# Layer B of a two-layer streaming encoder: head pair 0 turned by DMA like the others, turns issued behind the query copies, the sample's value product in another bank, inverse sums and scans later

## The chip, the cores and the metric

The kernel runs on one core of one Trainium2 chip. A core has a matrix engine (TensorE, "PE" in the profile, with its weight loads shown apart as "PEld"), three engines for elementwise work (VectorE "DVE", ScalarE "ACT", GpSimd "POOL") and SyncE ("SP"), which here issues nearly all DMAs, in order, from one queue. Each engine works through its own list of instructions and waits for the others by semaphores. The metric is the device time of one execution in microseconds; the time shown is the median of a few runs.

## The reference

Two layers with a residual; the second one (layer B) is where the change lies.

```python
def project(x, norm_g, w_in, q_g, k_g, n_heads, n_kv):
    h = rms_norm(x, norm_g)
    q, k, v, gate = split(h @ w_in)          # per head of 64
    return rms_norm(q, q_g), rms_norm(k, k_g), v, gate

def attend(q, k, v, bias, valid, sinks):
    s = q @ k.T * 64 ** -0.5 + bias
    s = where(valid, s, -1e30)
    p = softmax(s)                           # layer A has sinks in the sum
    return p @ v

def gated_attention_layer(...):
    o = attend(...)                          # prompt: in chunks of 64 frames
    y = x + (o * silu(gate)) @ w_out
```

The prompt has 2048 frames, the sample 64 frames with a cache of 256. The width is 1024. Layer A has 16 query heads over 2 key heads and sees the own chunk of 64 and 2 earlier ones; layer B has 16 heads of its own and sees the own chunk and 8 earlier ones, with a learned bias by clipped distance.

## The kernel before

**Tiling.** Layer A runs first, then layer B. Layer B goes through its heads in 8 head pairs (`hp` 0 to 7). Within a head pair it goes through nine units in the order 0 to 6, sample, 7: a prompt unit is 256 frames, two tiles of 128; the sample is one unit of 64. Each unit has a projection (q, k, v and gate of this head pair, on PE at L706 to L708) and an attention. The projections of a later unit are cut into small pieces by the class `Filler` and put between the steps of the attention, so that PE has work while the softmax of a step goes through DVE and ACT. Small jobs of DVE, ACT and POOL (the low halves of queries and keys, of values, the gate, the inverse sums, weight preparation) are kept in the class `Background`: `put` queues one, `share` runs a part of them after each step, `run` runs one at once because its result is wanted. `tick` counts the shares. A job that has run in a share is tied behind the newest `anchor` of its engine, an instruction of the current step's softmax.

**What sets the order.** PE's order is the order in which the program is written. The lists of the other engines and of SP are set by a scheduler from the dependences; `behind(a, b)` and the anchors add "not before b on this engine".

**One attention step** (`pipeline`, function `scores`) is one head `h` of one tile `i`. PE multiplies queries by keys into one of two "sb" banks of PSUM (L1487 the high halves, L1488 the low). DVE adds the bias and takes the negative maximum `nm` (L1491), ACT takes the exponential and its sum `sm` (L1500). The weights `p` then have to be turned, keys on partitions, for the product with the values:

- In head pairs 1 to 7 (`turned`) DVE first adds a constant to `nm` (L1496), ACT makes a 16-bit high half (L1545), POOL the low half (L1546), and SP turns both with one DMA transpose (L1554, tile `pt`), issued a step later. Four steps after the score PE multiplies them by the values (`turned_products`, L1648).
- In head pair 0, and for the sample, PE transposes `p` in blocks of 128x128 into an "sb" bank (L895 in `values`), ACT and DVE split the result (L867, L868), and PE multiplies by the values in `products` (L1687), for the sample in `sample_outputs` (L1606, L1607).

After both heads, `gates` transposes the gate times the inverse sums (`G`, L895) and `finish` gathers the output: ACT L1302, DVE L1306, POOL L1307 and a store (L1314). Products and output stand in the one "o" bank. The sample's product also takes the "o" bank, after `run_all` of two lists of small jobs.

`queries` prepares the next unit: PE transposes q and k into the one "tp" bank, ACT writes the high halves (L1426, L1427), DVE the low halves (L1438, L1442), and SP copies the queries to the other half of the partitions (L1431, `q<-q`; issued by `flush` at the next step). `inverse` takes the reciprocal of the four sums (DVE L1519) and multiplies it into the gate (POOL L1530). It is put in the background when the scores of a unit's last step are written, and runs at the latest in `gates`.

**Scans.** Weights are scaled to 16 bit by their largest value, found a head pair ahead: a block of 512 columns is loaded (L182) and reduced (DVE L175); L231 and L190 collect the maxima.

**Head pair 0 alone** also makes the normed rows x1 for all head pairs: loads (L571), a row scale (POOL L587), ACT L590 and POOL L591 split them in two halves, and a store (L602) puts them in memory, from where the other head pairs read them.

## Time and profile before

| | before |
|---|---|
| median of three runs | 2196.76 us (2193.1 to 2198.49) |
| the profiled execution, its own time | 2200.77 us |
| its span in the profile | 2199.0 us |
| POOL L591 (x1 halves, whole span) | 184.1 us in 144 |
| POOL L1546 (low halves of turned weights) | 283.5 us in 224 |
| DMA transposes pt<-values | 224 |

A row of waits says which engine waited for what: total, times and longest in us. A row of a group gives busy time and the mean length of one in ns, then the idle time before it and who ended it. A timeline row gives start, length, engine, line and operation, and in brackets the idle time before it with its releaser. A DMA issue row ends with the median time from issue to landing. Head pair 0 of layer B's attention runs from 901.80 to 1062.60 us, the seven others from there to 2045.

### The profile page before, as it was taken

Reading aid. Unit: us, or ns where it says so; the run is one execution under the profiler, and the core shown is the slowest. Engines: PE = TensorE matmul, PEld = TensorE weight load, DVE = VectorE, ACT = ScalarE, POOL = GpSimd, SP = SyncE. Lnnn points to the kernel's source line nnn. Section 1 sums busy time; section 2 is a strip of 40 time slices with the busy share of each in tenths; the row PEclk is TensorE's granted clock in tenths of the full one; section 3 lists DMA queues with packets and bytes.
Section 4 is the critical chain, followed back from the end, with each engine's and each line's share of the span. In section 5 each row is a group of like instructions: output and inputs, shape, how many; then the busy total and the mean of one; then the engine's idle time right before and its main releaser. Section 6 shows DMA issues by size and latency. Waiting matters only on the chain.

```text
span 2199.0 us, 40839 instructions
## 1 busy us (share of the span) xinstructions
PE 2074.1 (94%) x12951; PEld 1476.7 (67%) x12951; DVE 1503.6 (68%) x4049; ACT 1428.2 (65%) x3610; POOL 1149.4 (52%) x1621
## 2 busy tenths in 40 slices
PE   7999999999999999899998999989999899899899
PEld 6887788878879998455554555545555455456788
DVE  6668778667676456678676686776867867577542
ACT  6878878767786333566666676766767668577420
POOL 5554544434454355754566575665756667465000
PEclk9999999999999999999999999999999999999999
DMA  8756546766545677635488696786867969568663
GB/s 267 260 173 215 184 128 212 212 181 195 176 123 162 201 216 218 221 113 195 115 190 212 142 209 170 184 222 142 209 180 168 231 129 207 146 139 187 203 206 122
DMA packets 512120, 404.96 MB, mean 184 GB/s; under 512 B 303696, under 2 KB 449376, under 8 KB 511872
## 3 DMA queue, kind: packets, MB, share of 16 engines
q1 hardware_dynamic: 511904, 402.35, 67.5%
q8 instruction: 102, 1.67, 0.3%
q14 instruction: 114, 0.93, 0.1%
HBM read 257.59 MB, written 73.43 MB: 151 GB/s over the span
## 4 chain that ended last, share of the span: by engine, by line
PE 52%; DVE 15%; DMA 12%; ACT 8%; POOL 6%; issue 5%; SPq 2%; ACTq 0%; POOLq 0%; DVEq 0%
PE pj L706 8%; PE pj L708 8%; PE pj L707 8%; PE pj L1856 5%; PE pj L1858 5%; PE pj L1857 5%; DMA wraw<-in_w_in_b_dram 4%; DVE p L1491 2%; PE sa L895 2%; POOL values L1546 2%; PE o L1648 2%; DVE pa L811 2%; DMA xraw<-in_x_rows_dram 2%; PE tp L895 2%; DMA wraw<-in_w_o_b_dram 1%
## 5 line engine op out<-in xcount | busy, mean ns | idle before, releaser
L706 PE MATMUL pj<-wh,xx 128*128 128x512 f16 (+2 forms) x1648 | 647.5, 393 | 5.8 <-ACT pb L729 2.2
L708 PE MATMUL pj<-wh,xx 128*128 128x512 f16 (+2 forms) x1648 | 628.8, 382 | 0.6 <-POOL xx L591 0.6
L707 PE MATMUL pj<-wh,xx 128*128 128x512 f16 x1024 | 395.3, 386 | 0.8 <-DVE wh L496 0.8
L1500 ACT ACTIVATE p<-p,nm 128x640 f32<-128x640 f32 (+5 forms) x264 | 199.6, 756 | 272.2 <-DVE nm L1496 218.1
L1546 POOL TENSOR_TENSOR values<-p,values 128x640 f16<-128x640 f32 (+2 forms) x224 | 283.5, 1266 | 157.9 <-ACT values L1545 155.4
L1856 PE MATMUL pj<-xx,wh 128*128 128x264 f32 (+1 forms) x1024 | 290.8, 284 | 5.5 <-DVE res L1866 2.7
L1857 PE MATMUL pj<-xx,wh 128*128 128x264 f32 (+1 forms) x1024 | 287.9, 281 | 0.0
L1491 DVE CUSTOM_DVE_ANT_0 p<-sb,BT 128x640 f32<-128x640 f32 (+5 forms) x272 | 195.5, 719 | 64.8 <-PE sb L1488 61.4
L707 PE MATMUL pj<-wl,xx 128*128 128x512 f32 (+1 forms) x624 | 234.7, 376 | 2.9 <-DVE wl L496 2.8
L591 POOL TENSOR_TENSOR xx<-xraw,xx 128x528 fp32r<-128x528 f32 (+4 forms) x144 | 184.1, 1297 | 91.3 <-ACT xx L590 84.1
L806 POOL TENSOR_TENSOR f<-f,mhalf 128x4 f32<-128x4 f32 (+2 forms) x187 | 191.4, 1024 | 12.9
L1307 POOL TENSOR_TENSOR o<-gt,o 128x256 f32<-128x256 f32 (+1 forms) x132 | 106.1, 804 | 165.0 <-ACT p L1210 91.4
L708 PEld LDWEIGHTS <-xx 128*128 128x128 f16 x1024 | 101.8, 99 | 127.5 <-issue 9.6
L811 DVE TENSOR_TENSOR pa<-pa,f 128x256 f32<-128x256 f32 (+3 forms) x221 | 143.3, 648 | 37.1 <-POOL f L806 32.4
L1210 ACT ACTIVATE p<-p,nm 128x257 f32<-128x257 f32 (+2 forms) x272 | 134.3, 497 | 50.5 <-DVE nm L1204 44.5
L788 POOL TENSOR_TENSOR sq<-pa 128x256 f32<-128x256 f32 (+2 forms) x187 | 114.3, 611 | 99.1 <-ACT pa L742 61.2
L706 PEld LDWEIGHTS <-xx 128*128 128x128 f16 x1024 | 101.8, 99 | 86.0 <-issue 5.7
L707 PEld LDWEIGHTS <-xx 128*128 128x128 f16 x1024 | 101.6, 99 | 81.7 <-issue 6.5
L1545 ACT CAST values<-p 128x640 f16<-128x640 f32 (+2 forms) x224 | 147.3, 658 | 6.5 <-DMA pt<-values 0.7
L1858 PE MATMUL pj<-xx,wl 128*128 128x264 f32 x512 | 145.4, 284 | 1.0 <-DVE wl L489 1.0
L1204 DVE CUSTOM_DVE_ANT_0 p<-sa,BT,nsink 128x256 f32<-128x256 f32 (+2 forms) x272 | 117.4, 468 | 38.6 <-PE sa L895 30.8
L1858 PE MATMUL pj<-xx,wh 128*128 128x264 f16 x512 | 142.1, 277 | 0.1
(273 smaller groups left out, 5032.0 us busy)
## 6 DMA issues: line engine op xcount, KB each, us to landing
xx<-xsb SPq DMA_DIRECT2D x112, 512.0 KB, 4.3
xx<-xsa SPq DMA_DIRECT2D x88, 512.0 KB, 4.9
xraw<-oga SPq DMA_DIRECT2D x64, 264.0 KB, 3.6
xraw<-ogb SPq DMA_DIRECT2D x64, 264.0 KB, 4.0
xsa<-xx SPq DMA_DIRECT2D x32, 512.0 KB, 4.1
wl<-in_w_in_b_dram SPq DMA_DIRECT2D x64, 256.0 KB, 4.9
wraw<-in_w_in_b_dram SPq DMA_DIRECT2D x56, 256.0 KB, 4.4
xraw<-in_x_dram SPq DMA_DIRECT2D x40, 256.0 KB, 4.0
```

Of the source, the lines that this page charges most:

```text
L591: nc.gpsimd.tensor_tensor(lo, rv, wide(hi), op=ALU.subtract)
L706: nc.tensor.matmul(ps[:n, :C], xh, wh, start=k == 0, stop=False)
L707: nc.tensor.matmul(ps[:n, :C], xh, wl, start=False, stop=False)
L708: nc.tensor.matmul(ps[:n, :C], xl, wh, start=False, stop=k == KC - 1)
L806: nc.gpsimd.tensor_tensor(fv, fv, mhalf[:n, :H], op=ALU.pow)
L811: nc.vector.tensor_tensor(sv, sv, fv.unsqueeze(2).to_broadcast([n, H, HD]), op=ALU.mult)
L1491: mi = nc.vector.tensor_tensor_reduce(out=p[r, :nk], in0=S[r, o : o + nk], in1=b, op0=ALU.add, op1=ALU.min, scale=1.0, scalar=3e38, accum_ ...
L1500: ex = nc.scalar.activation(p[:n, :nk], p[:n, :nk], AF.Exp, scale=-1.0, bias=it.nm[:n, c : c + 1], accum_out=it.sm[:n, c : c + 1],)
L1546: lo = nc.gpsimd.tensor_tensor(two[:, :, 1, :], pv, two[:, :, 0, :], op=ALU.subtract)
L1856: nc.tensor.matmul(ps[:, :OT], wh, oh, start=k == 0, stop=False)
L1857: nc.tensor.matmul(ps[:, :OT], wh, ol, start=False, stop=False)
L1858: nc.tensor.matmul(ps[:, :OT], wl, oh, start=False, stop=k == KC - 1)
```

## The change

1. `turned` no longer asks for `hp > 0`: the prompt units of head pair 0 are turned by DMA too. With it the delay `late` in `then`, the bank in `gates` and one scale become the same for all head pairs. In head pair 0, 140 PE transposes of 128x128 fall away, and 168 products move from L1687 to L1648; 32 DVE low halves (L868) go and 32 constants (L1496) come; ACT has 32 copies in place of 32 splits; POOL gets 32 subtractions (12 of the 16 per head at 640 columns), SP 32 DMA transposes.
2. A turn is tied behind the last copy of queries on SP.
3. The sample's product goes to the "tp" bank, and so no longer runs the two lists first.
4. `inverse` is put in the background one share later, after the last step's own.
5. The reductions of `scan` are tied behind the anchor of their engine. A background job may ask for a number of shares to pass (`wait`); the low half of v and the product of the gate ask for two.

```diff
--- before.py
+++ after.py
@@ -172,9 +172,11 @@
     def scan(i=None, keep=0):
         while len(pending) > keep:
             j, raw = pending.pop(0)
-            nc.vector.tensor_reduce(
+            r = nc.vector.tensor_reduce(
                 most[:, j : j + 1], raw, axis=AX.X, op=ALU.max, apply_absolute_value=True
             )
+            if r.ins.engine in bg.anchors:
+                behind(r.ins, bg.anchors[r.ins.engine])
             scanned.append(j)
         if i is not None:
             raw = t("wraw", [P, 512], WB) if keep else t("scan", [P, 512], 1)
@@ -237,7 +239,7 @@
         powers(row[:, h : h + 1], e, r)
         times(o[:, 0:1], r, WB_)
         times(o[:, 1:2], e, 1 / (HB * WB_))
-        times(o[:, 2:3], e, 0.5 / VB if h > 0 and len(TURNED) == 2 else 0.5 / (VB * PB))
+        times(o[:, 2:3], e, 0.5 / VB)
 
     def input_scales(h):
         everywhere(h, row[:, 20:23])
@@ -389,9 +391,10 @@
             self.queue, self.anchors, self.cost, self.lazy = [], {}, 0.0, False
             self.tick = 0
 
-        def put(self, cost, fn, urgent=False, lazy=False, weights=False, after=None):
+        def put(self, cost, fn, urgent=False, lazy=False, weights=False, after=None, wait=1):
             it = Item()
             it.fn, it.cost, it.urgent, it.weights, it.after = fn, cost, urgent, weights, after
+            it.wait, it.born = wait, self.tick
             if urgent:
                 self.queue.insert(sum(q.urgent for q in self.queue), it)
             else:
@@ -432,7 +435,9 @@
                     break
                 if it.fn is None or it.weights and most == 0:
                     continue
-                if it.after is not None and (it.after.fn is not None or it.after.tick == self.tick):
+                if it.after is not None and it.after.fn is not None:
+                    continue
+                if self.tick < it.wait + (it.after.tick if it.after is not None else it.born):
                     continue
                 most -= it.weights
                 budget -= it.cost
@@ -750,7 +755,7 @@
                 vh[:, :, HD:P], v, c, vh[:, :, 0:HD], op0=ALU.mult, op1=ALU.subtract
             )
 
-        held["rest"].append(bg.put(0.2, low, True))
+        held["rest"].append(bg.put(0.2, low, True, wait=2))
         held["evac"] = nc.scalar.activation(g, ps[:, 384:512], AF.Identity, scale=C_B(hp)).ins
         return a
 
@@ -833,7 +838,7 @@
         if not apart:
             return [bg.put(0.3, curve)]
         first = bg.put(0.2, curve)
-        return [first, bg.put(0.2, product, after=first)]
+        return [first, bg.put(0.2, product, after=first, wait=2)]
 
     def split_v(n, src, vt):
         sv = src.rearrange("p (h d) -> p h d", d=HD)
@@ -1428,7 +1433,7 @@
 
             def copies():
                 for hh, rows in enumerate(halves):
-                    load(wide(q1[hh][halves[1 - hh]]), wide(q1[hh][rows]))
+                    held["copy"] = load(wide(q1[hh][halves[1 - hh]]), wide(q1[hh][rows])).ins
 
             if it not in its[-2:]:
                 held["later"].append(copies)
@@ -1505,14 +1510,8 @@
             if turned(it, h):
                 parts(it, i, h, p, nk // P)
             if c == w - 1:
-                def fn():
+                if u == NU:
                     inverse(it, n, w)
-
-                item = bg.put(0.8, fn, True)
-                if u != NU:
-                    it.inverse = item
-                    return
-                bg.run(item)
 
         def inverse(it, n, w):
             u, T, tiles = it.unit
@@ -1535,7 +1534,7 @@
                 )
 
         def turned(it, h):
-            return it.unit[0] != NU and it.hp > 0 and h in TURNED
+            return it.unit[0] != NU and h in TURNED
 
         def parts(it, i, h, p, m):
             held["turn"] = r = (held["turn"] + 1) % 3
@@ -1551,9 +1550,10 @@
             if i == 0:
                 it.ph[h] = t("pt", [P, 2 * HALF], 2, F16)
             m = two.shape[1]
-            nc.sync.dma_start_transpose(
+            turn = nc.sync.dma_start_transpose(
                 it.ph[h][:, HALF * i : HALF * i + m].rearrange("p (c q) -> p c q", q=P), two
             )
+            behind(turn.ins, held["copy"])
 
         def values(it, i, h, short):
             u, T, tiles = it.unit
@@ -1581,13 +1581,15 @@
             ))
 
         def then(it, i, h):
-            late = it.hp > 0 and len(TURNED)
+            late = len(TURNED)
             if it.unit[0] == NU:
                 return [
                     (1, "values", (it, i, h)), (2 + late, "call", lambda: sample_outputs(it)),
                     (3 + late, "call", lambda: sample_turned(it)),
                 ]
             last = i == len(it.unit[2]) - 1
+            if (i, h) == (1, 1):
+                it.inverse = bg.put(0.8, lambda: inverse(it, P, 4), True)
             if turned(it, h):
                 two = it.two[i]
                 todo = [(1, "call", lambda: turn_p(it, i, h, two))]
@@ -1600,7 +1602,7 @@
             return psum("o", 512, 1)
 
         def sample_outputs(it):
-            O = o_bank()
+            O = tp_bank()
             for c in range(3):
                 vs = VS[:, c].rearrange("p h d -> p (h d)")
                 nc.tensor.matmul(O[:, 0:256], it.ph[0][:, c, 0:P], vs, start=c == 0, stop=False)
@@ -1657,7 +1659,7 @@
             u, T, tiles = it.unit
             n = tiles[0][2]
             bg.run(it.inverse)
-            GT = psum_b("sb", 1024, 2) if it.hp and len(TURNED) else tp_bank()
+            GT = psum_b("sb", 1024, 2)
             for e, (_, t0, _) in enumerate(tiles):
                 transpose(GT[:, t0 : t0 + n], it.G[:n, e * P : (e + 1) * P])
             it.gt = gate_t(GT[:, :T].rearrange("p (j s) -> p j s", j=1), T, G_B(it.hp))
```

SyncE's list in head pair 0, in the middle of its units, before (L571 loads and L602 stores x1, L1431 copies queries, L182 loads weights for a scan, L1314 stores an output):

```order
L571 DMA xraw_12564<-x_98 128x2x256
L1431 DMA q_2514_12428<-q_2514_12428 64x256 x2
L182 DMA wraw_12774<-in_w_o_b_dram 128x512
L1314 DMA ogb<-o_2511_12409 128x256
L571 DMA xraw_12805<-x_98 128x2x64
L602 DMA xsb<-xx_12586 128x2048
```

The same place with the change, where the lines are five higher (L576 and L607 are x1, L1436 the copies, L1553 a turn):

```order
L1436 DMA q_2497_12394<-q_2497_12394 64x256 x2
L607 DMA xsb<-xx_12333 128x2048
L1553 DMA_TRANSPOSE pt_12376<-values_11645 128x10x128
L576 DMA xraw_12523<-x_98 128x2x256
L184 DMA wraw_12708<-in_w_o_b_dram 128x512
L1553 DMA_TRANSPOSE pt_12474<-values_11645 128x10x128 x2
L1319 DMA ogb<-o_2508_12471 128x256
L1553 DMA_TRANSPOSE pt_12595<-values_11645 128x10x128
L576 DMA xraw_12746<-x_98 128x2x64
```

The turns stand behind the copies and between the loads and stores of x1.

VectorE's list at the end of head pair 2, just ahead of the sample's product, before:

```order
L1438 SCALAR_TENSOR_TENSOR q_1_111<-tp_17245,qf,q_3402_17250 64x256
L1442 SCALAR_TENSOR_TENSOR KB<-tp_17245,kf,KB 64x256
L175 TENSOR_REDUCE most<-wraw_17661 128x1
L231 TENSOR_TENSOR most<-most,gain 128x8
L190 TENSOR_REDUCE top<-most 128x1
L1491 ISA p_17321,nm_17146<-sb_17320,BT 128x640
L1491 ISA nm_17146 128x1
L811 TENSOR_TENSOR pa_17238<-pa_17238,f_17268 128x256
L1306 TENSOR_TENSOR o_3414_17310<-o_17192,o_3414_17310 64x256 x2
L831 SCALAR_TENSOR_TENSOR pb_17108<-sq_17291,pb_17108 128x128
```

And with the change (L1447 is the low half of the keys, L1496 the bias and maximum, L816 and L836 small jobs of the projection, L1311 the last read of the "o" bank):

```order
L1447 SCALAR_TENSOR_TENSOR KB<-tp_17121,kf,KB 64x256
L1496 ISA p_17197,nm_17022<-sb_17196,BT 128x640
L1496 ISA nm_17022 128x1
L816 TENSOR_TENSOR pa_17114<-pa_17114,f_17143 128x256
L1311 TENSOR_TENSOR o_3366_17186<-o_17066,o_3366_17186 64x256 x2
L175 TENSOR_REDUCE most<-wraw_17015 128x1
L836 SCALAR_TENSOR_TENSOR pb_16984<-sq_17167,pb_16984 128x128
```

The reduction of the scan (L175) moved from ahead of the step's softmax to behind it and behind the last read of the "o" bank; the collecting of the maxima is no longer here.

GpSimd's list around one unit of head pair 0, before (L587, L591 x1; L788, L805, L806 row norms; L1530 inverse sums into the gate):

```order
L1530 TENSOR_TENSOR G_12261<-pb_11760,sm_12078 128x128 x2
L788 TENSOR_TENSOR sq_12312<-pa_12294 128x256
L587 TENSOR_TENSOR xraw_12324<-xraw_12324,rows_12320 128x512
L587 TENSOR_TENSOR xraw_12328<-xraw_12328,rows_12320 128x512
L591 TENSOR_TENSOR xx_12349<-xraw_12324,xx_12349 128x512
L805 TENSOR_TENSOR f_12313<-f_12313,small 128x4
L806 TENSOR_TENSOR f_12313<-f_12313,mhalf 128x4
L591 TENSOR_TENSOR xx_12349<-xraw_12322,xx_12349 128x512
L591 TENSOR_TENSOR xx_12357<-xraw_12326,xx_12357 128x512
L591 TENSOR_TENSOR xx_12357<-xraw_12328,xx_12357 128x512
L788 TENSOR_TENSOR sq_12445<-pa_12418 128x256
```

And with the change (L592, L596 x1; L793, L810, L811 row norms; L1545 the low half of the weights to be turned):

```order
L592 TENSOR_TENSOR xraw_12304<-xraw_12304,rows_12300 128x512
L592 TENSOR_TENSOR xraw_12308<-xraw_12308,rows_12300 128x512
L810 TENSOR_TENSOR f_12295<-f_12295,small 128x4
L1545 TENSOR_TENSOR values_11645<-p_12277,values_11645 128x5x128
L596 TENSOR_TENSOR xx_12325<-xraw_12302,xx_12325 128x512
L596 TENSOR_TENSOR xx_12333<-xraw_12306,xx_12333 128x512
L596 TENSOR_TENSOR xx_12325<-xraw_12304,xx_12325 128x512
L811 TENSOR_TENSOR f_12295<-f_12295,mhalf 128x4
L1545 TENSOR_TENSOR values_11645<-p_12345,values_11645 128x5x128
L596 TENSOR_TENSOR xx_12333<-xraw_12308,xx_12333 128x512
L793 TENSOR_TENSOR sq_12410<-pa_12384 128x256
L810 TENSOR_TENSOR f_12411<-f_12411,small 128x4
```

Four low halves per unit now stand among the halves of x1 (two of them in these rows).

## The prediction

> **What bounds the kernel now.** I read the page first, for the engines' shares and the chain of waits; then the busy time of each engine by stretch, one for each head pair of layer B; then the waits of TensorE (PE) in the seven head pairs 1 to 7; last the timeline around the places that the change touches. The page:
>
> ```profile
> span 2199.0 us, 40839 instructions
> PE 2074.1 (94%) x12951; PEld 1476.7 (67%) x12951; DVE 1503.6 (68%) x4049; ACT 1428.2 (65%) x3610; POOL 1149.4 (52%) x1621
> PE 52%; DVE 15%; DMA 12%; ACT 8%; POOL 6%; issue 5%; SPq 2%; ACTq 0%; POOLq 0%; DVEq 0%
> ```
>
> PE is busy 94% of the span, and the chain that ended last runs through it for 52%. The time can fall in two ways: PE gets less to do, or its stalls (6%, and what hangs on them) get shorter. The change does the first in head pair 0 and means to do the second in the others.
>
> The next view gives busy time by stretch; the columns are the stretch, its length, PE, weight loads, DVE, ACT and POOL busy (instructions), the granted clock, DMA share and GB/s. The rows are head pair 0, its units 0 to 4, its rest (units 5, 6, the sample, 7), and the same rest of head pair 1.
>
> ```profile
> 901.80:1062.60 160.80, 149.58 (x918) 90.69 (x916) 124.04 (x296) 105.57 (x264) 89.48 (x125) 0.99 0.50 160
> 901.80:993.20 91.40, 83.93 (x519) 50.55 (x516) 68.93 (x166) 59.40 (x153) 60.16 (x77) 1.00 0.45 143
> 993.20:1062.60 69.40, 65.66 (x399) 40.14 (x400) 55.11 (x132) 46.17 (x112) 29.33 (x48) 0.98 0.57 182
> 1142.00:1204.80 62.80, 55.23 (x319) 31.28 (x318) 46.71 (x122) 43.26 (x107) 38.84 (x54) 0.97 0.90 219
> ```
>
> Head pair 0 is the longest, and PE fills 93% of it: 149.58 of 160.80. In units 0 to 4 POOL is already at 66% (60.16 of 91.40), since it also splits the normed rows x1 there. The waits of PE in head pairs 1 to 7 (total us, times, longest):
>
> ```profile
> PE sb L1487 <- DMA q<-q: 14.5, 11, 2.6
> PE o L1606 <- DVE o L1306: 12.9, 7, 2.3
> PE sb L1487 <- DVE nm L1491: 12.8, 8, 2.5
> PE tp L205 <- DVE KB L1442: 5.9, 1, 5.9
> PE sb L1487 <- ACT gt L1292: 3.5, 5, 1.2
> PE o L895 <- POOL o L1613: 2.9, 1, 2.9
> ```
>
> The first three are what the change's smaller edits aim at: 40.2 us in all.
>
> **Head pair 0, turned by DMA.** The weights of its two turned heads no longer pass through PE. Rows for the price: the transposes in the stretch of head pair 0, then PE in that stretch on the old product line and, in head pair 2, on the line that takes its place (same columns as above, PE and weight loads only), then the subtraction by which POOL makes the low half before a turn, at each size.
>
> ```profile
> L895 PE MATMUL sb<-ident,p 128*128 128x128 f32 x143 | 26.1, 278 | 2.3 <-DVE pl L868 1.7 <-DVE nm L1491 0.6
> 901.80:1062.60 160.80, 23.69 (x156) 16.11 (x156) 0.99 0.50 160
> 1204.80:1345.10 140.30, 17.96 (x168) 15.42 (x168) 0.98 0.79 183
> L1546 POOL TENSOR_TENSOR values<-p,values 128x640 f16<-128x640 f32 x168 | 238.2, 1418 | 130.8 <-ACT values L1545 128.4 <-issue 1.3 <-DMA q<-q 0.5
> L1546 POOL TENSOR_TENSOR values<-p,values 128x512 f16<-128x512 f32 x14 | 16.4, 1172 | 15.5 <-ACT values L1545 15.5
> L1546 POOL TENSOR_TENSOR values<-p,values 128x384 f16<-128x384 f32 x14 | 13.1, 932 | 3.2 <-ACT values L1545 3.1
> L1546 POOL TENSOR_TENSOR values<-p,values 128x256 f16<-128x256 f32 x14 | 9.6, 686 | 4.0 <-ACT values L1545 4.0
> L1546 POOL TENSOR_TENSOR values<-p,values 128x128 f16<-128x128 f32 x14 | 6.3, 449 | 4.4 <-ACT values L1545 4.4
> ```
>
> A transpose occupies PE 26.1/143 = 0.183 us, and 140 of them go: 80 in units 0 to 4 (1, 2, 3 and 4 blocks in the first four tiles, 5 in each of the other six, times two heads), 60 in units 5 to 7. A product costs 23.69/156 = 0.152 us on the old line and 17.96/168 = 0.107 on the new; 168 change over, 96 and 72.
>
> Units 0 to 4: PE falls by 80 x 0.183 + 96 x 0.045 = 19.0 to 65. POOL gets two subtractions of each small size, 2 x (0.449 + 0.686 + 0.932 + 1.172) = 6.5, and 12 large, 17.0: it goes from 60.16 to 83.7. So POOL, not PE, becomes the bound, and 83.7 us of work lie in a stretch that took 91.4. What share can the engine that sets the pace keep here? PE, which sets it now, keeps 83.93/91.40 = 92%; by that row POOL needs 83.7/0.92 = 91.0. I take this: gain 0.4 us. Bounds: 100% gives 83.7 (gain 7.7); 80%, halfway between POOL's present 66% and PE's share, gives 104.6 (loss 13.2).
>
> Units 5 to 7 and the sample: PE falls by 60 x 0.183 + 72 x 0.045 = 14.2 to 51.5; POOL rises by 12 x 1.418 to 46.3. Neither fills the stretch. Head pair 1, turned in this way, took 62.8 us there with 55.23 on PE, so I take 63: gain 6.4. Bounds: 0 and, at PE's 92%, 69.4 - 56 = 13.4.
>
> ACT trades a split copy for a split copy; 32 DVE instructions of the low half go (its load is 124 of 160.8, no bound), and 32 tiny ones come. These I cost at nothing: ACT and DVE have some quarter of the stretch free, and DVE's load falls. SP gets 32 more transposes; see the rivals. Head pair 0: **-7 us**, from -21 to +13.
>
> A rule of the Trainium skill speaks against the POOL sum. "GPSIMD Engine Reference", section "1. Specifications", has POOL's interfaces to SBUF shared with VectorE, with contention when a DVE instruction has two SBUF inputs. By it the added 23.5 us of POOL would stretch DVE work beside it; with DVE at 75% of units 0 to 4 that moves the sum only if DVE then passes POOL.
>
> **The sample's value product in the transposes' bank.** The timeline of head pair 4:
>
> ```profile
> 1616.00 0.49 DVE L1442 SCALAR_TENSOR_TENSOR KB<-tp,kf,KB 64x256 f16<-64x256 f32 x1
> 1616.52 0.69 DVE L175 TENSOR_REDUCE most<-wraw 128x1 f32<-128x512 f32 x1
> 1618.81 0.84 DVE L1306 TENSOR_TENSOR o<-o,o 64x256 f32<-64x256 f32 x2
> 1619.79 0.49 PE L1606 MATMUL o<-VS,ph 128*128 128x256 f32 x1 [2.09 <-DVE o L1306]
> ```
>
> PE comes to the product at 1617.70 (1619.79 less the 2.09 it waits) and stands until DVE has emptied the "o" bank in L1306, which is queued behind a scan (L175) and its sums. The "tp" bank, which the product now uses, was last read by L1442, done at 1616.49, 1.2 us before PE arrives. So the wait goes and no other takes its place: **-12.9 us** over seven head pairs (L1606 above). Unknown is who next wants the "tp" bank: the next queries' transposes, several steps on, behind some 2 us of product and its evacuation; bounds 0 and -12.9.
>
> With the stall goes what follows on it. Granted clock (the number after POOL's busy) just after the product in head pairs 1, 3 and 4, then after a softmax stall in units 5 of head pairs 2, 4 and 5:
>
> ```profile
> 1200.10:1203.40 3.30, 3.26 (x11) 2.10 (x12) 1.40 (x7) 2.44 (x7) 2.29 (x6) 0.50 0.45 112
> 1480.00:1483.30 3.30, 3.30 (x11) 2.09 (x12) 1.34 (x7) 2.44 (x7) 2.42 (x6) 0.50 0.43 108
> 1619.90:1623.30 3.40, 3.40 (x12) 1.94 (x13) 1.25 (x7) 2.40 (x7) 2.59 (x6) 0.50 0.37 100
> 1295.60:1302.40 6.80, 5.79 (x16) 2.42 (x17) 6.72 (x18) 6.62 (x15) 5.02 (x5) 0.50 0.98 248
> 1575.50:1578.90 3.40, 3.40 (x11) 1.20 (x9) 3.39 (x8) 3.24 (x7) 2.61 (x3) 0.50 0.89 245
> 1715.40:1718.80 3.40, 3.40 (x10) 1.38 (x10) 3.40 (x9) 3.22 (x9) 3.10 (x3) 0.50 0.93 235
> ```
>
> For 3.4 us at half clock the work of 1.7 us gets done: three after the product cost **-5.1 us**, the softmax ones 13.6/2 = 6.8, of which I count half, **-3.4**.
>
> Here the Trainium skill would have it otherwise. "TensorE: Matmul & The Clock Gate", section "Part 1: The HAM clock gate (the "warmup" mystery)", has the clock halved after at least one idle window of about 3.4 us. By that rule a 2.09 us stall halves nothing, and removing it returns no clock: these 8.5 us would not come. The trace differs: 2.09 us of stall at 1619.79 is followed by 0.50.
>
> **Scans and inverse sums later.** A scan that DVE starts waits for its weights and holds back the softmax behind it:
>
> ```profile
> 1291.00 0.69 DVE L175 TENSOR_REDUCE most<-wraw 128x1 f32<-128x512 f32 x1 [2.02 <-DMA wraw<-in_w_in_b_dram]
> ```
>
> The reciprocal sums likewise move from before the next scores to a share after the step. The change puts scans behind what DVE does for the current step. Of the 12.8 us of PE's waits on the softmax (nm L1491) I take 8; bounds 0 (they wait for other things as well: DVE's load is unchanged) and 12.8. **-8 us.** What may be late next is the scale made from the scan; it is needed a head pair later, and 3 us do not matter to it.
>
> **Turns behind the query copies.** The copies q<-q keep PE waiting for 14.5 us. In the sample's case it is not a turn that holds them but ACT:
>
> ```profile
> 1458.82 0.47 ACT L1426 ACTIVATE q<-tp,qf 64x256 f16<-64x256 f32 x1
> 1461.28 0.32 PE L1487 MATMUL sb<-KA,q 128*128 128x384 f16 x1 [2.20 <-DMA q<-q]
> q<-q SPq DMA_DIRECT2D x250, 32.0 KB, 2.7
> ```
>
> ACT writes q until 1459.29, and the copies (2.7 us from issue to landing, the last row) can start no sooner; the order on SP cures nothing here. I take a fifth, **-3 us**, bounds 0 and -14.5. What stands behind a turn on SP (weight loads, stores) moves back with it.
>
> Two small jobs, the low half of v and the product in the gate, may now start a step later. I cost them at nothing: they run beside PE's projections and are wanted a unit or more later. Without that cover each would show as a wait of PE on its result, and no such wait is among the rows above.
>
> **Sum for head pairs 1 to 7.** 12.9 + 5.1 + 8 + 3.4 + 3 = 32.4. Not all passes through: PE that runs ahead meets the waits that stay (L205 5.9, gt 3.5, L1613 2.9, the rest of q<-q 11.5: 23.8 together). I let two thirds pass: -21.6. With head pair 0, -28.6. Outside layer B nothing that PE does is changed. The profiled execution took 2200.77 us with a span of 2199.0, 4 us over the median of 2196.76; its own time would come to 2172, and from the median the forecast is **2168**.
>
> **Rivals.**
> *POOL as a worse bound in head pair 0 (slower).* The place is units 0 to 4; POOL alternates there between splits that wait for ACT and DVE, and if it keeps only the 66% it keeps now, 83.7 us take 127: +35.6. Less 6.4 and 21.6 that is 2204. It decides against the change from a share of 70% down (83.7/0.70 = 119.6, +28). For it speaks that x1 loads in SP's queue wait for POOL:
>
> ```profile
> SPq L571 <- POOL xx L591: 41.7, 9, 10.4
> ```
>
> so delays of POOL feed back through SP into the turns. Against it: an engine with a queue full of ready work waits less, and the large subtraction's own idle time above, 130.8, arose where POOL had little else to do.
> *The waits come back elsewhere.* If a third passes instead of two, head pairs 1 to 7 give 10.8: 2179. For it: PE and DVE are coupled every step, and DVE at 68% has no less to do. Against: the product's stall sits in PE's own order, where nothing else is late.
> *Turns come late.* A turn now stands behind the copies on SP, which wait for ACT. In head pair 4, unit 4:
>
> ```profile
> 1554.84 1.35 SPq L1554 DMA_TRANSPOSE pt<-values  x1
> 1561.55 1.26 PE L1648 MATMUL o<-pt,values 128*128 128x256 f16 x12
> pt<-values SPq DMA_TRANSPOSE x224, 3.8
> ```
>
> The turn lands at 1558.6, 2.9 us before its use. Copies that wait for less than that cost nothing, more becomes a new wait of PE on the turn; with half of the 21.6 eaten so, 2179, and with head pair 0's gain gone too, 2186. Before, PE has no such wait among its larger ones, which speaks against.
> *The clock returns nothing.* Then 12.9 + 8 + 3 = 23.9, two thirds 15.9, with 7 for head pair 0: 2174. The Trainium skill's rule above is this case; the six half-clock rows speak against it.
> *The change misses its aim:* copies late from ACT, scans replaced by others, so that only the product's 12.9 counts; that lies within the second rival.
>
> **How the numbers follow.** Forecast 2168 (own range 2150 to 2180): 0.42. POOL worse: 0.17. Waits come back: 0.20. Turns late: 0.13. No clock gain: 0.08. A measurement of this kernel can tell about 0.3%, 6.6 us: same is 2190.2 to 2203.4. Slower is most of the POOL case (0.12) and the end of the late turns (0.02); same takes 0.03 of POOL, 0.05 of the late turns and 0.05 of the returning waits; the rest, 0.73, is faster. The range that holds eight in ten reaches from 2147 (all of the 32.4 passes, head pair 0 gains 17) to 2202.
>
> **What would show it.** Right: head pair 0 takes some 154 us, with POOL above 85% in its first 91; PE's wait of the sample product on DVE is gone, its waits on the softmax fall below 6 us, the copies' stay near 11; fewer stretches at clock 0.50. Wrong: head pair 0 longer than 165 us with POOL idle between splits; PE waiting in the turned products on pt; a new wait for the "tp" bank after the sample; head pairs 1 to 7 shorter by less than 8 us together.

## The result, and the profile after

The changed kernel takes 2163.86 us (median of five runs, 2161.53 to 2166.7); beside it the kernel before took 2194.36 (five runs, 2193.1 to 2198.49). The ratio is 0.9855, 95% interval 0.9842 to 0.9869: 30.5 us less, where the prediction had 28.6. The sum came out; its terms did not. Head pair 0, which was to gain 7 us, lost 15, and head pairs 1 to 7 gained 46.5 instead of 21.6.

The page of the kernel after: span, engines, chain.

```profile
span 2164.2 us, 40771 instructions
PE 2040.5 (94%) x12811; PEld 1456.0 (67%) x12811; DVE 1488.2 (69%) x4049; ACT 1429.6 (66%) x3610; POOL 1188.4 (55%) x1653
PE 62%; DVE 12%; ACT 8%; DMA 6%; issue 6%; POOL 6%; SPq 1%; POOLq 0%; ACTq 0%; DVEq 0%
```

PE is as full as before (94%), busy 33.6 us less, and the chain runs through it for 62% instead of 52%: fewer steps of it are waits for DVE and DMA.

Busy time by stretch, columns as in the prediction. First the kernel after: head pair 0, its units 0 to 4, its rest, and head pairs 1 to 7 together.

```profile
901.80:1077.40 175.60, 136.99 (x758) 75.27 (x756) 113.03 (x290) 106.66 (x263) 128.24 (x153) 0.91 0.76 190
901.80:1010.90 109.10, 77.70 (x428) 42.87 (x427) 61.52 (x168) 60.21 (x152) 81.10 (x94) 0.89 0.65 158
1010.90:1077.40 66.50, 59.30 (x332) 32.40 (x331) 51.52 (x124) 46.45 (x111) 47.14 (x60) 0.95 0.95 242
1077.40:2011.20 933.80, 891.98 (x5430) 522.83 (x5431) 687.21 (x1879) 680.79 (x1695) 611.94 (x815) 0.99 0.82 188
```

And head pairs 1 to 7 of the kernel before:

```profile
1062.60:2042.90 980.30, 909.58 (x5394) 525.17 (x5391) 690.70 (x1872) 679.89 (x1694) 612.99 (x812) 0.97 0.76 178
```

Head pair 0 is 14.8 us longer (160.8 before), all of it in units 0 to 4: 109.1 for 91.4. Head pairs 1 to 7 are 46.5 us shorter: of that 17.6 is PE busy time at the same work, which is clock (0.97 to 0.99), and 28.9 is idle time of PE (70.7 to 41.8). The last 3.1 us of the 34.8 by which the span fell lie behind head pair 7: PE's wait of 2.9 us in L895 for POOL's `o`, the sample's output of the last head pair, stands there in the kernel before, and the kernel after has no such wait there.

PE's waits after the change in head pair 0 (total, times, longest):

```profile
PE tp L900 <- DVE pa L816: 28.1, 4, 10.6
PE pj L712 <- DVE wh L501: 3.6, 2, 2.2
```

and in head pairs 1 to 7:

```profile
PE sb L1492 <- DVE nm L1496: 11.2, 8, 1.9
PE sb L1478 <- DMA QS<-QS: 7.5, 4, 2.5
PE tp L207 <- DVE KB L1447: 6.9, 1, 6.9
PE o L900 <- POOL o L1615: 4.8, 6, 1.6
PE sb L1492 <- DMA q<-q: 4.1, 3, 2.0
```

The wait of the sample's product (12.9 us) is gone. The wait for the copies q<-q fell from 14.5 to 4.1, the one on the softmax hardly, from 12.8 to 11.2; the sample's own query copies (QS) now take 7.5. In head pair 0 stands a new wait that was not there: PE's transposes of q and k wait for DVE's row norm in L816.

The timeline of unit 2 of head pair 0 after the change, one of the four (start, length, engine, line, operation; in brackets the idle time before and its releaser):

```profile
945.73 0.20 POOL L810 TENSOR_TENSOR f<-f,small 128x4 f32<-128x4 f32 x1
945.88 1.39 POOL L1545 TENSOR_TENSOR values<-p,values 128x640 f16<-128x640 f32 x1
947.24 3.37 POOL L596 TENSOR_TENSOR xx<-xraw,xx 128x512 f16<-128x512 f32 x3
950.57 1.00 POOL L811 TENSOR_TENSOR f<-f,mhalf 128x4 f32<-128x4 f32 x1
951.60 1.61 DVE L816 TENSOR_TENSOR pa<-pa,f 128x256 f32<-128x256 f32 x1 [6.89 <-POOL f L811]
953.36 0.66 PE L900 MATMUL tp<-ident,pa 128*128 128x128 f32 x2 [7.70 <-DVE pa L816]
```

The small power L811 (1.00 us) needs L810, done at 945.93, but stands on POOL behind a low half of the new kind (L1545) and three halves of x1 (L596) until 950.57. DVE waits 6.89 us for it, PE 7.70. The two other long stalls, which end at 929.39 and 981.25, are of the same kind: in the three, 4.5 to 6.3 us of POOL's work stand between the two powers, 1.2 to 1.4 us of it a low half and the rest nearly all x1. In the kernel before the two powers follow each other within 0.1 us in all ten projections of units 0 to 4, for example:

```profile
939.12 0.65 POOL L805 TENSOR_TENSOR f<-f,small 128x4 f32<-128x4 f32 x1
939.84 1.33 POOL L806 TENSOR_TENSOR f<-f,mhalf 128x4 f32<-128x4 f32 x1
```

And the clock is low behind the stalls: busy time and granted clock (the number after POOL's busy) in the 3.4 us behind this one, behind the longest (10.58 us, it ends at 981.25) and behind the one in unit 1, which is 8.40 us long.

```profile
953.30:956.70 3.40, 3.34 (x11) 1.74 (x12) 1.56 (x5) 1.66 (x4) 1.50 (x2) 0.50 0.42 134
981.20:984.60 3.40, 3.35 (x12) 1.77 (x13) 1.58 (x5) 1.66 (x4) 0.14 (x1) 0.59 0.70 214
929.30:932.70 3.40, 3.31 (x12) 1.78 (x13) 1.96 (x7) 2.41 (x7) 1.68 (x3) 0.50 0.57 209
```

The timeline has the one in unit 1 at its end:

```profile
929.39 0.66 PE L900 MATMUL tp<-ident,pa 128*128 128x128 f32 x2 [8.40 <-DVE pa L816]
```

### The profile page after: what moved, and what is told of

It reads as the page before. It is cut to its first block, busy times and chain, and to the rows that moved or that the text cites. A ratio compares the mean times of both kernels' runs of the same rounds, so it can differ in the third digit from the quotient of the medians.

```text
span 2164.2 us, 40771 instructions
## 1 busy us (share of the span) xinstructions
PE 2040.5 (94%) x12811; PEld 1456.0 (67%) x12811; DVE 1488.2 (69%) x4049; ACT 1429.6 (66%) x3610; POOL 1188.4 (55%) x1653
## 4 chain that ended last, share of the span: by engine, by line
PE 62%; DVE 12%; ACT 8%; DMA 6%; issue 6%; POOL 6%; SPq 1%; POOLq 0%; ACTq 0%; DVEq 0%
PE pj L711 11%; PE pj L713 11%; PE pj L712 11%; PE pj L1858 4%; PE pj L1860 4%; PE pj L1859 4%; PE o L1650 3%; PE sa L900 2%; PE tp L900 2%; PE sb L1492 2%; PE sb L1493 2%; DVE p L1496 2%; POOL values L1545 2%; DVE wh L501 1%; DVE pa L816 1%
## 5 line engine op out<-in xcount | busy, mean ns | idle before, releaser
L1545 POOL TENSOR_TENSOR values<-p,values 128x640 f16<-128x640 f32 (+4 forms) x256 | 322.8, 1263 | 209.3 <-ACT values L1544 205.7
L1496 DVE CUSTOM_DVE_ANT_0 p<-sb,BT 128x640 f32<-128x640 f32 (+5 forms) x272 | 196.7, 723 | 138.0 <-PE sb L1493 130.0
L596 POOL TENSOR_TENSOR xx<-xraw,xx 128x528 fp32r<-128x528 f32 (+4 forms) x144 | 183.5, 1293 | 88.7 <-ACT xx L595 81.0
L811 POOL TENSOR_TENSOR f<-f,mhalf 128x4 f32<-128x4 f32 (+2 forms) x187 | 191.2, 1024 | 11.1
L816 DVE TENSOR_TENSOR pa<-pa,f 128x256 f32<-128x256 f32 (+3 forms) x221 | 144.3, 654 | 76.9 <-POOL f L811 72.3
L1544 ACT CAST values<-p 128x640 f16<-128x640 f32 (+4 forms) x256 | 168.3, 658 | 10.8 <-DMA pt<-values 4.9
L793 POOL TENSOR_TENSOR sq<-pa 128x256 f32<-128x256 f32 (+2 forms) x187 | 114.6, 613 | 108.8 <-ACT pa L747 70.1
L1650 PEld LDWEIGHTS <-values 128*128 128x128 f16 x1344 | 123.6, 98 | 39.0 <-issue 1.1
L1650 PE MATMUL o<-pt,values 128*128 128x256 f16 (+1 forms) x1344 | 144.0, 255 | 1.0 <-ACT o L1622 0.9
```

The costliest lines, as they stand in the source:

```text
L596: nc.gpsimd.tensor_tensor(lo, rv, wide(hi), op=ALU.subtract)
L811: nc.gpsimd.tensor_tensor(fv, fv, mhalf[:n, :H], op=ALU.pow)
L1496: mi = nc.vector.tensor_tensor_reduce(out=p[r, :nk], in0=S[r, o : o + nk], in1=b, op0=ALU.add, op1=ALU.min, scale=1.0, scalar=3e38, accum_ ...
L1545: lo = nc.gpsimd.tensor_tensor(two[:, :, 1, :], pv, two[:, :, 0, :], op=ALU.subtract)
L1650: nc.tensor.matmul(it.O[:, h * T + q0 : h * T + q1_], held["VH"][:, kt, h], x, start=kt == kb and not low, stop=kt == tb and low == 1,)
```

## The experiments

All were timed in three rounds beside the kernel before on the same chip. The kernel before differs a little from one job to the next (2194 to 2200 us), so two kernels of different jobs compare better by their differences to it; where both are told, the first is by medians, the second by these differences. The last two columns are the lengths of the stretches (us) in the one profiled run of each.

| kernel | median us | before beside it | ratio (95%) | head pair 0 | head pairs 1 to 7 |
|---|---|---|---|---|---|
| changed kernel | 2163.86 | 2194.36 | 0.9855 (0.9842 to 0.9869) | 175.6 | 933.8 |
| hp0_by_pe | 2151.84 | 2198.29 | 0.9789 (0.9748 to 0.9830) | 165.2 | 932.8 |
| hp0_low_dve | 2152.64 | 2198.29 | 0.9787 (0.9747 to 0.9826) | 166.0 | 931.4 |
| hp0_late_units | 2150.01 | 2198.29 | 0.9776 (0.9743 to 0.9810) | 156.9 | 937.0 |
| hp0_one_head | 2163.82 | 2197.32 | 0.9851 (0.9816 to 0.9885) | 170.9 | 936.5 |
| product_o_bank | 2181.67 | 2198.29 | 0.9921 (0.9893 to 0.9950) | 175.4 | 949.3 |
| turns_free | 2168.39 | 2200.27 | 0.9862 (0.9839 to 0.9885) | 175.3 | 942.0 |
| inverse_early | 2162.34 | 2200.27 | 0.9834 (0.9810 to 0.9857) | 171.3 | 939.1 |
| scan_free | 2179.86 | 2200.27 | 0.9912 (0.9893 to 0.9931) | 177.5 | 949.7 |
| waits_one | 2185.08 | 2200.27 | 0.9933 (0.9918 to 0.9948) | 187.2 | 946.0 |
| low_v_one | 2183.00 | 2197.32 | 0.9941 (0.9925 to 0.9957) | 187.8 | 940.5 |
| before_product | 2178.62 | 2197.32 | 0.9917 (0.9889 to 0.9944) | 161.6 | 968.9 |
| before_part5 | 2168.56 | 2197.32 | 0.9872 (0.9835 to 0.9909) | 163.9 | 947.8 |

### Head pair 0: who loses the 15 us

**hp0_by_pe**: part 1 undone.

```diff
-            return it.unit[0] != NU and h in TURNED
+            return it.unit[0] != NU and it.hp > 0 and h in TURNED
```

(with `late`, the bank in `gates` and the scale as before)

> The changed kernel with part 1 alone undone: head pair 0 goes back to transposes on PE, all else stays. Theory (head pair 0 lost 15 us to POOL, and what head pairs 1 to 7 gained has nothing to do with it): head pair 0 falls from 175.6 to about 160 us, head pairs 1 to 7 stay within 5 us, total about 2149. Rival (the time lost in head pair 0 is work done earlier that head pairs 1 to 7 are spared): head pairs 1 to 7 get longer by 10 us or more, total 2160 to 2168.

Measured: head pair 0 at 165.2, head pairs 1 to 7 at 932.8, against 933.8. The rival falls: nothing that head pair 0 loses comes back later. Undoing part 1 makes the changed kernel 12 us faster by medians and 16 by differences, where the theory had 15; head pair 0 came to 165 and not 160. Most of the difference goes with part 5: put alone into the kernel before (before_part5, below), it lengthens head pair 0 from 160.8 to 163.9.

**hp0_low_dve**: the same work, other engine.

```diff
-            lo = nc.gpsimd.tensor_tensor(two[:, :, 1, :], pv, two[:, :, 0, :], op=ALU.subtract)
+            lo = (nc.gpsimd if it.hp else nc.vector).tensor_tensor(two[:, :, 1, :], pv, two[:, :, 0, :], op=ALU.subtract)
```

> The changed kernel with the low halves of the turned weights of head pair 0 (32 subtractions) made by DVE, not POOL. Theory (PE waits in head pair 0 for the small power of the row norm, which stands on POOL behind low halves and x1 work): POOL loses some 40 us of work there, PE's wait on DVE pa falls from 28.1 to under 8 us, head pair 0 takes 150 to 162 us, total 2140 to 2152. Rival 1 (turns are late on SP, or DMA is too busy): head pair 0 stays at 170 us or more, total 2160 or more. Rival 2 (DVE, with 26 us more, is the next bound): the wait moves to the softmax, head pair 0 163 to 170 us, total 2152 to 2160.

PE's largest wait in head pair 0 of this kernel, then its units 0 to 4 by busy time:

```profile
PE tp L900 <- DVE pa L816: 13.2, 3, 6.8
```

```profile
903.60:1001.80 98.20, 79.60 (x427) 43.09 (x426) 76.50 (x187) 60.17 (x152) 62.83 (x74) 0.91 0.70 176
```

The turns, SP and the DMAs are as in the changed kernel, and the stretch falls from 109.1 to 98.2 us, the wait from 28.1 to 13.2; the total falls to 2152.64, inside Rival 2's 2152 to 2160 at its lower end. Turns or DMA as the main cause are out. The theory has the direction, not the size: it had the wait under 8 us and head pair 0 at 162 at most, and that came to 166.0. POOL's low halves are the larger part of the loss; with them moved, DVE has 76.50 of 98.20 (61.52 of 109.10 before the move), and three stalls of the same kind stay; the wait has not moved to the softmax, as Rival 2 had it.

**hp0_late_units**: PE turns units 0 to 4, DMA units 5 to 7.

```diff
-            return it.unit[0] != NU and h in TURNED
+            return it.unit[0] != NU and (it.hp > 0 or it.unit[0] >= 5) and h in TURNED
```

(both kinds take the constant in `nm`, and products of the first kind come two steps after the step)

> The changed kernel with units 0 to 4 of head pair 0 turned by PE as before, units 5 to 7 by DMA. Theory (the loss is in units 0 to 4, where POOL also splits x1): that stretch is back at some 92 us, from 109, the rest stays at 63 to 67, total about 2147. Rival (the turn by DMA costs wherever head pair 0 uses it): units 5 to 7 take 70 us or more and the total is above 2152.

Busy time in units 0 to 4 and in the rest of head pair 0:

```profile
903.00:993.10 90.10, 82.60 (x515) 50.61 (x513) 71.17 (x186) 58.96 (x152) 58.62 (x75) 1.00 0.44 141
993.10:1059.90 66.80, 58.92 (x325) 32.27 (x324) 50.09 (x125) 46.96 (x112) 45.37 (x55) 0.95 0.89 226
```

As the theory had it: units 0 to 4 are back at 90.1, with clock 1.00; units 5 to 7, where POOL has no x1, keep 66.8 with the turn by DMA (69.4 in the kernel before). The loss belongs to units 0 to 4. It has the lowest median of the study, 48.3 us below the kernel before, 2.2% (interval 1.9 to 2.6), though hp0_by_pe can't be told from it.

**hp0_one_head**: in units 0 to 4 one head by DMA, the other by PE.

```diff
-            return it.unit[0] != NU and h in TURNED
+            return it.unit[0] != NU and (it.hp > 0 or it.unit[0] >= 5 or h == 1) and h in TURNED
```

> The changed kernel with head pair 0 shared out in units 0 to 4: one head turned by DMA, the other by PE; units 5 to 7 by DMA. By the theory that POOL's load (all turned) and PE's (none turned) are the two bounds there, each gets half: PE some 74 us and POOL some 72 in that stretch, which then takes 84 to 89 us (109.1 with both turned, 90.1 with none), total 2143 to 2149. If any low half in POOL's queue holds back the row norm that PE waits for: 95 us or more, total 2153 or more.

PE's largest wait in head pair 0, then units 0 to 4:

```profile
PE tp L900 <- DVE pa L816: 16.1, 3, 6.0
```

```profile
903.50:1005.70 102.20, 83.75 (x467) 48.28 (x465) 64.72 (x176) 59.71 (x152) 68.07 (x82) 0.90 0.51 145
```

The half load did not take half a stretch: 102.2, above the middle of 90.1 and 109.1. POOL is busy only 67% of it, and still PE waits 16.1 us for the norm. So it isn't POOL's sum alone that bounds the stretch but its order. The expectation has the number right and the reason only in part: in none of the three stalls does a low half stand between the two powers. It is x1 work alone, 2.2 to 4.6 us of it, here in the stall of 5.72 us:

```profile
969.73 0.19 POOL L810 TENSOR_TENSOR f<-f,small 128x4 f32<-128x4 f32 x1
969.88 3.42 POOL L596 TENSOR_TENSOR xx<-xraw,xx 128x512 f16<-128x512 f32 x3
973.26 1.00 POOL L811 TENSOR_TENSOR f<-f,mhalf 128x4 f32<-128x4 f32 x1
```

So what the turn by DMA costs here is not only the low halves: with it the list has two to four pieces of x1 between two powers that stand side by side in the kernel before and have at most one piece between them with part 1 undone (hp0_by_pe). Why the scheduler orders it so, no run shows.

### Head pairs 1 to 7: which part gains the 46.5 us

**product_o_bank** undoes part 3 (`O = o_bank()` in `sample_outputs`).

```diff
-            O = tp_bank()
+            O = o_bank()
```

> The changed kernel with part 3 alone undone: the sample's product takes the o bank again. By the prediction's sum the wait (12.9 us in seven head pairs) and the half clock behind it (5.1) come back: 2182 if all of it counts, 2176 if two thirds do. Rival (the waits cured come back elsewhere anyway): a third, 2170 or less, with other waits of PE shorter by as much.

Head pairs 1 to 7 at 949.3 (+15.5), the span behind them 3 us longer; the total 17.8 us more by medians, 13.9 by differences. The theory's two values were 18 and 12; a third (6) is out. PE's wait, in head pairs 1 to 7 of this kernel, is back:

```profile
PE o L1608 <- DVE o L1311: 11.5, 7, 2.0
```

**turns_free** undoes part 2.

```diff
-            behind(turn.ins, held["copy"])
```

> The changed kernel with part 2 alone undone: turns are no longer held behind the query copies on SP. Outside part 3 the change took 31 us off head pairs 1 to 7 (980.3 before, 949.3 with part 3 undone), three times the 9.6 that the prediction let through for parts 2, 4 and 5. Theory P (the prediction's split): part 2 is worth 2 to 4 us, head pairs 1 to 7 at 936 to 938 us, total 2166 to 2168. Theory S (SP's order is the main cause, since PE's wait on the copies fell from 14.5 to 4.1 us): head pairs 1 to 7 at 944 us or more, that wait above 10 us, total 2174 or more.

The profiled run has 942.0, but the median is 2168.39 and the ratio 0.9862 (0.9839 to 0.9885) lies on that of the changed kernel: part 2 can't be told from nothing by the times, and Theory S falls by them (2174 or more) and by the wait on q<-q, 7.5 us where it had over 10.

**inverse_early** undoes part 4.

```diff
-            if (i, h) == (1, 1):
-                it.inverse = bg.put(0.8, lambda: inverse(it, P, 4), True)
...
             if c == w - 1:
-                if u == NU:
+                def fn():
                     inverse(it, n, w)
+                item = bg.put(0.8, fn, True)
+                if u != NU:
+                    it.inverse = item
+                    return
+                bg.run(item)
```

> The changed kernel with part 4 alone undone: the inverse sums are put in the background when the scores are written. DVE's wait for the exponential's sums in L1519, 39.7 us in 45 waits before, is not among the larger waits after the change. Theory I (DVE stood in this wait with the next softmax behind it): head pairs 1 to 7 at 944 us or more, DVE's wait on ACT p above 25 us, total 2174 or more. Theory P: part 4 is a share of the 8 us for the softmax waits: 935 to 939 us, total 2165 to 2169.

2162.34, ratio 0.9834 (0.9810 to 0.9857), overlapping that of the changed kernel: no difference that can be told, though the profiled run has 939.1. In head pairs 1 to 7 DVE does stand 37.3 us in that wait again:

```profile
DVE sm L1524 <- ACT p L1505: 37.3, 41, 1.0
```

It is spread over 41 times of at most 1.0 us. PE waits for its result twice, in the scores of the sample (6.4 us), but the total isn't longer for it. Theory I falls.

**scan_free** undoes the tie of the scans.

```diff
-            if r.ins.engine in bg.anchors:
-                behind(r.ins, bg.anchors[r.ins.engine])
```

> The changed kernel without the tie of the scans' reductions to the anchor. DVE waited 55.4 us for weights in L175 before and does not after. Theory D (these waits cost PE): head pairs 1 to 7 at 942 us or more, PE's wait on the softmax above 14 us, total 2172 or more. Theory P: 2 to 5 us, 936 to 939 us, total 2166 to 2169. If DVE merely waits elsewhere: within 2 us of the changed kernel.

PE's waits in head pairs 1 to 7, then one of DVE's:

```profile
PE sb L1490 <- DVE nm L1494: 20.1, 12, 3.0
PE tp L898 <- DVE pa L814: 7.5, 5, 1.7
...
PE sb L1490 <- DMA q<-q: 6.9, 7, 1.6
```

```profile
DVE most L175 <- DMA wraw<-in_w_o_b_dram: 23.9, 9, 4.5
```

949.7 (+15.9), and the total 16.0 more by medians, 10.1 by differences: Theory D. DVE waits for weights again, and PE for DVE: 20.1 us on the softmax against 11.2, 7.5 on the row norm against none.

**waits_one** sets both waits back to one share, **low_v_one** only that of the low half of v.

```diff
-        held["rest"].append(bg.put(0.2, low, True, wait=2))
+        held["rest"].append(bg.put(0.2, low, True))
...
-        return [first, bg.put(0.2, product, after=first, wait=2)]
+        return [first, bg.put(0.2, product, after=first)]
```

> The changed kernel without the two waits of two shares (the low half of v, the product in the gate). The prediction has them at nothing: head pairs 1 to 7 within 2 us of 933.8, total 2162 to 2166. Rival (DVE's wait of 25.1 us for pb in L749 and 23.4 for sq in L831, which are smaller after, held the softmax back): 940 us or more, total 2170 or more.

> The changed kernel with the wait of the low half of v alone back at one share; the gate's product keeps its two. Undoing both cost 12.2 us in head pairs 1 to 7 and 11.6 in head pair 0. If the low half of v is the one that matters (DVE waits for ACT's pb in L754, 8.0 us in head pairs 1 to 7 with the wait, 16.9 without): head pairs 1 to 7 at 941 or more, total 2176 or more. If it is the gate's product (DVE's wait on ACT's sq, 6.1 against 19.4): within 4 us of 933.8, total 2162 to 2168.

21.2 and 19.1 us more by medians, 15.3 and 16.2 by differences: the rival of the first, and for the second the low half of v, which by the totals accounts for all of it (its stretch of 940.5 lies just under the 941 expected). What the prediction had at nothing is worth as much as the product. With both waits undone PE's wait on the copies in head pairs 1 to 7, 4.1 us in the changed kernel, is

```profile
PE sb L1492 <- DMA q<-q: 11.0, 9, 3.3
```

In the profiled run of low_v_one head pair 0 is 12.2 us longer and head pairs 1 to 7 are 6.7. Its PE waits on the softmax in head pairs 1 to 7:

```profile
PE sb L1492 <- DVE nm L1496: 17.4, 13, 2.1
```

and on the row norm in head pair 0:

```profile
PE tp L900 <- DVE pa L816: 36.1, 6, 9.9
```

The first is 6.2 us more than the 11.2 of the changed kernel, about the loss there. A chain that fits: the low half needs ACT's pb, and DVE that takes it up a share earlier stands for it in front of the softmax. But the trace shows only a part of it: DVE's wait for pb is 12.1 us here against 8.0, while its wait for POOL's power of the row norm (in L816) grows from 38.0 to 56.0. That the low half's place costs this is shown; how, in the main, is argued. In head pair 0 the second grows from 28.1 to 36.1; by which chain the low half lengthens it was not tried.

**before_product** and **before_part5** put one part alone into the kernel before (the diffs of parts 3 and 5).

```diff
 def sample_outputs(it):
-            O = o_bank()
+            O = tp_bank()
```

> The kernel before with part 3 alone: the sample's product in the tp bank. The prediction's sum for it is 12.9 + 5.1 us, two thirds of that 12; undoing it in the changed kernel cost 15.5 in head pairs 1 to 7. If it stands by itself: head pairs 1 to 7 from 980.3 to 962 to 968 us, total 12 to 18 below the kernel before. If its gain needs the other parts (PE that is released only meets the next wait): 974 us or more, total less than 7 below.

> The kernel before with part 5 alone: scans tied to the anchor, two jobs with a wait of two shares. Undone one at a time in the changed kernel these cost 15.9 and 12.2 us in head pairs 1 to 7. If they stand by themselves and add: head pairs 1 to 7 from 980.3 to about 952, total 25 to 30 below the kernel before. If they only keep what other parts gain: 966 or more, total less than 15 below. By the prediction's split (8 of waits and 3.4 of clock, two thirds through): 972, total 8 below.

18.7 and 28.8 us below the kernel before: both stand by themselves, and together they are 47.5, about what head pairs 1 to 7 and the span behind them gained (46.5 + 3.1). In the profiled run the product's 11.4 in head pairs 1 to 7 are a little under the 12 to 18 expected, with 3 more behind them. Busy time in head pairs 1 to 7 with part 5 alone, then PE's waits there:

```profile
1065.60:2013.40 947.80, 894.84 (x5399) 519.80 (x5397) 697.55 (x1880) 678.61 (x1694) 609.50 (x814) 0.98 0.79 185
```

```profile
PE o L1611 <- DVE o L1311: 12.4, 7, 2.8
PE sb L1492 <- DVE nm L1496: 12.2, 7, 2.3
...
PE sb L1492 <- DMA q<-q: 5.2, 7, 1.9
```

Part 5 alone takes PE's wait on the copies from 14.5 to 5.2, with the order on SP untouched, and leaves the wait on the softmax at 12.2. PE's busy time falls by 14.7 us (909.58 to 894.84) at the same work.

## Why the prediction was right, and where it was wrong

**Total**: 28.6 forecast, 30.5 measured. That the two are so close is luck: head pair 0 was off by 21.8 us to one side and head pairs 1 to 7 by 24.9 to the other, each by more than the term itself.

**Units 0 to 4 of head pair 0: wrong.** The step is "by that row POOL needs 83.7/0.92 = 91.0". PE's share was taken for POOL's. POOL's work was sized right (83.7 forecast, 81.10 busy), but it keeps 74% of the stretch: 109.1 us, 18 more than the forecast and 4.5 beyond the upper bound of 104.6. PE runs pieces of a projection that are ready and are laid out by hand; POOL's list mixes three chains, and a small member of one can stand behind large ones of the others. hp0_one_head shows it with half the load: 67% busy, and the wait is there. So the rival "POOL as a worse bound" came true in its place, at a share just above its turning point of 70%, and by another path than the one named for it: not SP's loads, but the power of the row norm, for which DVE and then PE wait. It did not make the kernel slower because head pairs 1 to 7 gained twice the 21.6 that had been let through.

**Units 5 to 7: right way, half the size.** 63 forecast, 66.5 measured, 69.4 before; of the 6.4 us, 2.9 came. POOL's work is as forecast (46.3 and 47.14), what PE is spared is not: its busy time was to fall to 51.5 here and to 65 in units 0 to 4, and it fell to 59.30 and 77.70. The lower clock (0.95 and 0.89, against 0.98 and 1.00 before) explains a part of that; the rest stays open.

**The product: right, and in full.** 12.9 + 5.1 = 18.0 stands against 18.7 measured with the part alone (interval 12 to 24), and 13.9 to 17.8 when it is undone. With the part alone PE's busy time in head pairs 1 to 7 falls by 5.9 us (909.58 to 903.67), where 5.1 were forecast for the clock. The bank was free as read, and behind the product of head pairs 1, 2 and 3 the clock now stands at 1.00:

```profile
1208.00:1211.40 3.40, 3.40 (x22) 2.02 (x21) 3.35 (x9) 0.90 (x5) 2.09 (x3) 1.00 0.47 102
1341.00:1344.40 3.40, 3.26 (x19) 1.54 (x17) 3.34 (x10) 1.52 (x5) 1.43 (x3) 1.00 0.63 134
1472.20:1475.60 3.40, 3.28 (x19) 1.56 (x17) 3.34 (x10) 1.50 (x5) 1.45 (x3) 1.00 0.63 133
```

**"I let two thirds pass": wrong.** Put in alone, the product brought about the whole of its sum (two thirds, 12, lie at the edge of the interval) and part 5 more than twice its own. The waits that stay (L207 6.9, POOL o 4.8) did not take in what was freed; only the sample's query copies, 1.2 before and 7.5 after, took some.

**Scans: right mechanism; part 5 as a whole too small, and the copies booked under the wrong part.** The 8 us were to come out of PE's wait on the softmax (nm). Undoing the tie of the scans puts 8.9 us back there (scan_free), and 7.5 on the row norm, which had no term. Yet between the two kernels the wait on the softmax fell by only 1.6. What part 5 alone cut is the wait for the copies, from 14.5 to 5.2, and the prediction had booked that under part 2. It had itself read that ACT, not SP, held the copies up; the right question was what holds ACT up. It is the two waits of two shares more than the scans: the copies' wait is 11.0 with the two undone and 6.9 with the tie undone. That DVE's delay reaches them through ACT fits a fall of ACT's own wait for DVE's nm (218.1 to 187.2 us in head pairs 1 to 7 with part 5 alone), but was not followed step by step. For the clock 3.4 were forecast; PE's busy time fell by 14.7 with part 5 alone.

**The low half of v "at nothing": wrong.** No wait of PE on its result was among the rows, which is why it was put at nothing; but its cost shows in other waits than PE's on its result. One is DVE's own wait for ACT's pb, with the softmax queued behind it. In the waits of DVE in head pairs 1 to 7 it stood before the change as

```profile
DVE values L749 <- ACT pb L754: 25.1, 32, 1.9
```

and after it as

```profile
DVE values L754 <- ACT pb L759: 8.0, 13, 1.1
```

With the low half alone set back it is 12.1, so it carries only a part of the cost. The product in the gate, put at nothing too, is worth nothing that the totals can tell (2.1 us by medians, none by differences).

**Turns behind the copies: nothing**, where 2 to 3 us were forecast; within what the times can tell. The rival of late turns didn't come: no wait of PE on pt is among the larger ones. **Inverse sums: nothing** that the times can tell.

**The signs.** Of those named for being right, the product's wait did go and the clock did rise in head pairs 1 to 7 (0.97 to 0.99); POOL above 85%, a wait on the softmax below 6 us and a wait for the copies near 11 did not come (74%, 11.2 and 4.1). Of those for being wrong, head pair 0 did pass 165 us, and POOL waited 11.0 us there, in units 0 to 4, for ACT's half of the split.

The rival "the clock returns nothing" falls with the rows above, and with 17.6 us of PE's busy time. The Trainium skill, "TensorE: Matmul & The Clock Gate", section "Part 1: The HAM clock gate (the "warmup" mystery)", halves the clock after an idle window of about 3.4 us. The stalls of 8.40 and 7.70 us in head pair 0, with 0.50 behind them, agree with it; the 2.09 us stall of the kernel before, with 0.50 behind it too, does not.

## What to carry to other kernels

Cost a move to another engine by the order of that engine's list, not by its free time: ask which small instruction, awaited by the bound engine, will now stand behind large ones, new or old, and by how much. When an in-order engine waits inside a low-priority job, look at what is queued behind it, not at who wants the job's result; the loss can show several engines further on, here partly as a wait for a copy. And count a stall of the matrix engine together with the half clock behind it.

## What was not expected of the hardware

A DVE instruction beside POOL's low halves can take nearly four times its length. In the kernel after, L816 on the same shape, first with POOL idle, then while POOL ran L1545 (951.54 to 952.93):

```profile
935.47 0.42 DVE L816 TENSOR_TENSOR pa<-pa,f 128x256 f32<-128x256 f32 x1
...
951.54 1.39 POOL L1545 TENSOR_TENSOR values<-p,values 128x640 f16<-128x640 f32 x1
951.60 1.61 DVE L816 TENSOR_TENSOR pa<-pa,f 128x256 f32<-128x256 f32 x1 [6.89 <-POOL f L811]
```

The Trainium skill, "GPSIMD Engine Reference", section "1. Specifications", has the two engines share their interfaces to SBUF, with contention for DVE instructions with two SBUF inputs. The rows agree: 1.2 us more, right on the path for which PE waited. They are no single case: in layer B's eight head pairs of the kernel after, L816 has this shape 125 times. The 51 of them with no POOL instruction beside them took 0.41 to 0.43 us each; 24 took over 1.3 us, each with POOL at work, and in 22 that work was L1545. Nor is it new: the kernel before has 21 over 1.3 us, 19 of them beside the low half in L1546. But POOL at work doesn't always slow it: others beside it took 0.41 too.
